# The out-projection of a hybrid encoder step: product halves in sequence, transpositions between them

## The chip, the cores and the metric

The kernel runs on one core of a Trainium2 chip. A core has five engines with one in-order queue each: TensorE (matmuls and transpositions, PE in the profile), VectorE (DVE), ScalarE (ACT), GpSimd (POOL) and SyncE (SP), which here issues all the DMAs. Matmul results land in PSUM, which has eight banks of 128 x 512 f32 values; ScalarE and VectorE carry them out of it. The metric is the device time of one execution in microseconds (us), as the median over runs.

## The reference, cut to what matters

One layer of a streaming encoder is applied to 1024 prompt frames and to 32 frames of a running stream, 1056 tokens of 1024 features. A mixer with three groups of heads (GLA, HGRN2, mLSTM) gives the concatenation `cat`; the out-projection, a norm, the residual, and a feed-forward block with a causal convolution follow:

```python
def run_trunk(x, states, params):                      # one layer, cut
    h, st_new = mixer(rms_norm(x, g_mix_pre[l]), ...)
    x = x + rms_norm(h, g_mix_post[l])
    h, ffn_buf = conv_ffn(rms_norm(x, g_ffn_pre[l]), ...)
    x = x + rms_norm(h, g_ffn_post[l])

def mixer(...):                                        # its end
    cat = jnp.concatenate([o_a, o_b, o_c], axis=-1)    # (B, T, 1024)
    return cat @ w_out, (...)                          # w_out (1024, 1024)

def conv_ffn(xn, buf, w_up, conv_w, conv_b, w_down):
    up = xn @ w_up
    up, buf = causal_dwconv(up, buf, conv_w, conv_b)
    gate, val = jnp.split(up, 2, axis=-1)
    return (jax.nn.gelu(gate, approximate=True) * val) @ w_down, buf
```

The recurrences of the three head groups run along the tokens, in chunks of 64; the new states are outputs too.

## The kernel before, in words

**Tiles of tokens.** The 1056 tokens form nine tiles: 0 to 7 with 128 tokens of the prompt each, and 8 with the 32 tokens of the running stream. The in-projection works in three groups, (0, 1, 2), (3, 4, 5) and (6, 7, 8). A matmul of two f32 operands is done as three matmuls of rounded high and low parts (`mm3`, lines 99 to 102), so one product of a token tile with a 1024 x 1024 matrix is 2 halves of 512 columns x 8 blocks of 128 rows x 3 = 48 matmuls.

**Mixers as side work.** `mixer` (line 704) is a generator: it traces the recurrences of one tile in some 15 steps, many small instructions on all engines, and yields between them. The mixers of a group run beside the stage that follows. `pump(k)` (line 1437) lets the side work advance by k steps; `merge(main, nmain, nside)` (line 1445) runs a main generator and, at each of its yields, pumps so many steps that nside steps are traced after nmain yields. The mixers of the last group, in the order 8, 6, 7, run beside the out-projection of the tiles 0, 1, 2, 3, 8, 4, 5 (`RING`, line 259). Each mixer needs the state of the one before it and shares its buffers, and writes its `cat` tile to DRAM; tile 7 keeps its own in SBUF.

**The out-projection of a tile.** `outproj` (line 1007) is a generator with four stages. The first loads the tile's cat (`load_cat`, line 261, tile ct) and residual (`load_res`, line 270, tile xr), and those of the next tile as well; it transposes cat into two PSUM banks, four blocks of 128 x 128 each (ctp, line 1031), and carries each out as a high part by ScalarE (ch, line 1035) and a low part by VectorE (cl, line 1036). These two have a raised priority. The second makes the product into two banks zp, block by block with the two halves alternating, and then ScalarE reads each bank twice, for the sum of squares (line 1066) and for a copy into the tile z (line 1067). The third is the norm, on GpSimd, VectorE and ScalarE (lines 1069 to 1086): scale by the norm and a gain (line 1076), add the residual (line 1077), store the sum (line 1078), square it (line 1081), scale again (line 1086). The fourth transposes the result into two banks (fxt, line 1100), which VectorE carries out with a gain (line 1105), and stores it for the up-projection (line 1108). Tile 0 also splits the out-projection's weights between its blocks (`out_weights`, line 994). The tiles 6 and 7 come after the others and have orders of their own.

**Buffers.** All of ctp, zp and fxt of the tiles 0 to 5 and 8 take their banks from one PSUM pool of three (`psb`, line 117). The tiles ct, xr and z of these tiles take theirs from a ring of seven slots in SBUF (`NRING`, line 256).

**The order.** `pipeline` (line 1113) takes the stages of successive tiles in turn: at place i the first stage of tile i, the fourth of the tile two places before, the third of the tile one place before, the second of tile i, with a yield behind each. A planner then sets the order of the instructions on each engine when the program is built: it follows the order of tracing as priority, its own estimates of durations, and the free buffers; a block under `tc.high_priority` counts as traced so much sooner. On the chip each engine then executes its list in that order.

**What follows.** Behind the out-projection come the up-projection (puy, pux, puw), whose operands VectorE and ScalarE prepare from the stored columns (T1l, B22l and others, line 1133), and the down-projection.

Of the kernel before, what the change touches and what calls it, by code (L numbers as in the profile page):

```python
# [8 lines left out]
F32 = mybir.dt.float32  # L9
# [3 lines left out]
AF = mybir.ActivationFunctionType  # L13
# [77 lines left out]
def body(ctx: ExitStack, tc: tile.TileContext, a: dict):  # L91
    nc = tc.nc
    act, dve, pool, pe, sp = nc.scalar, nc.vector, nc.gpsimd, nc.tensor, nc.sync
# [5 lines left out]
    def mm3(ps, lh, rh, first, last, **kw):  # L99
        pe.matmul(ps, lh[0], rh[0], start=first, stop=False, **kw)  # L100
        pe.matmul(ps, lh[0], rh[1], start=False, stop=False, **kw)  # L101
        return pe.matmul(ps, lh[1], rh[0], start=False, stop=last, **kw)  # L102
# [14 lines left out]
    psb = ctx.enter_context(tc.tile_pool(name="psb", bufs=3, space=PSUM))  # L117
# [25 lines left out]
    def xsrc(t0, n):  # L143
        return a["xp"][t0:t0 + n, :] if t0 < SEQ else a["xs"][t0 - SEQ:t0 - SEQ + n, :]
# [862 lines left out]
    def outproj(p2, W, u):  # L1007

        gm, woh, wol = W[:3]
        n = 128 if u < 8 else DEC  # L1010
        t0 = 128 * u
        load_cat(u)
        if u in RING:
            load_res(u)
            nxt = (RING + (6,))[RING.index(u) + 1]
            load_cat(nxt)
            if nxt in RING:
                load_res(nxt)
        ct = ct_of[u]
        chs = []  # L1020
        for hf in range(2):
            if u < 7 or u == 8:
                ps = psb.tile([128, 4, 128], F32, tag="big", name=f"ctp{u}{hf}")
            else:
# [3 lines left out]
                ps = both[:, hf]  # L1028
# [8 lines left out]
            if u == RING[0]:  # L1037
                halves[:] = ins
            chs += [(ch[:, k, :n], cl[:, k, :n]) for k in range(4)]
        yield  # L1040
        ss = p2.tile([128, 4], F32, tag="oss", name=f"oss{u}", bufs=2)
        pss = [psb.tile([128, 512], F32, tag="big", name=f"zp{u}{hf}") if u != 7 else
               upper[0].tile([128, 512], F32, tag="xw", name=f"zp{u}{hf}", bufs=4) for hf in range(2)]
        cs = [slice(512 * hf, 512 * hf + 512) for hf in range(2)]
        if u == 7:

            jk = jks[0]
            for hf in range(2):
                for k in range(8):
                    mm3(pss[hf], chs[k], (woh[:, k, cs[hf]], wol[:, k, cs[hf]]), k == 0, k == 7)  # L1050
                with tc.high_priority(offset=AHEAD):
                    kept["jk"] = act.activation(jk, pss[hf], AF.Square, accum_out=ss[:, hf:hf + 1])
        else:
            for k in range(8):
                if u == RING[0]:
                    next(W[3])
                for hf in range(2):
                    mm3(pss[hf][:n], chs[k], (woh[:, k, cs[hf]], wol[:, k, cs[hf]]), k == 0, k == 7)
                if k == 3 and u == 6:
                    yield  # L1060
        load_res(u)
        x = xr_of[u]
        if u != 7:
            z = (ring if u in RING else tail)[0](f"z{u}")
            for hf in range(2):
                act.activation(z[:n, cs[hf]], pss[hf][:n], AF.Square, accum_out=ss[:n, hf:hf + 1])
                act.copy(z[:n, cs[hf]], pss[hf][:n])
# [11 lines left out]
        if u == 7:  # L1079
            z = tail[0]("z7")  # L1080
# [356 lines left out]
    def pump(k):  # L1437
        while k > 0 and side:
            try:
                next(side[0])  # L1440
                k -= 1
            except StopIteration:
                side.pop(0)

    def merge(main, nmain, nside):

        done = 0
        for i, _ in enumerate(main):
            want = (i + 1) * nside // nmain
            pump(want - done)  # L1450
            done = want
# [6 lines left out]
    NMIX, NIN = 17, 12 + 2 + 24  # L1458
# [243 lines left out]
```

## Time and profile before

| | |
|---|---|
| time, median of 3 runs | 1419.99 us (1419.96 to 1420.18) |
| the profiled execution, its own time | 1421.18 us |
| its span | 1419.4 us |
| TensorE busy | 1368.0 us, 96% of the span |
| VectorE busy | 1009.2 us, 71% |
| ScalarE busy | 711.3 us, 50% |
| GpSimd busy | 281.9 us, 20% |

The profile is of one execution. Its page gives the busy time of each engine, groups of instructions by line, and the chain of waits. A row of a group reads: line, engine, operation, names of output and inputs, shapes, count, busy time, mean duration, idle time of the engine in front and what ended it. A row of the order in time reads: start, duration, engine, line, operation, names, and in brackets the idle time in front with its releaser. "x48" is a count. Line 1066 is the activation of line 1066; `mm3` gives the lines 100, 101 and 102, and `split` the lines 106 and 109, whoever calls them. The durations of matmuls overlap, so steps between starts tell the rate. The granted clock is that of TensorE as a share of full speed.

### The profile page before, as it was taken

To read this page: it belongs to the slowest core of one execution; us is meant where nothing else is said; L and a number is where in the kernel's file an instruction comes from. 1 tells how busy PE (TensorE), PEld (TensorE's weight loads), DVE (VectorE), ACT (ScalarE), POOL (GpSimd) and SP (SyncE) were. 2 spreads that over 40 slices of the span, in tenths; PEclk is the share of its full clock that TensorE was granted. 3 is DMA by queue.
4 is the path that set the end of the run, shared out by engine and by line. 5 is a ranking of instruction groups with operands and counts; after the bars stand their busy time and mean duration, and the time that the engine had idled before them with its cause. 6 is when DMAs were issued, how large, how long until landed. Compare 5 with 4: busy or idle time off the path is not lost.

```text
span 1419.4 us, 30029 instructions
## 1 busy us (share of the span) xinstructions
PE 1368.0 (96%) x11804; PEld 1253.1 (88%) x11804; DVE 1009.2 (71%) x1818; ACT 711.3 (50%) x1403; POOL 281.9 (20%) x461
## 2 busy tenths in 40 slices
PE   6989999999999998899899999999999999999998
PEld 5989889998888876767799999999999999988886
DVE  4795469758687667676798887788888875654644
ACT  4555447445474545333755545554455544533432
POOL 5531211224112223212131111111111110000100
PEclk9999999999999989999999999999999999999999
DMA  9599779776789753344412221221222156765652
GB/s 344 191 338 342 242 238 309 232 254 210 270 281 341 256 179 125 129 145 102 138 50 99 79 91 70 91 76 73 79 82 85 62 199 239 235 221 169 245 176 100
DMA packets 132581, 255.11 MB, mean 180 GB/s; under 512 B 27639, under 2 KB 78487, under 8 KB 132439
## 3 DMA queue, kind: packets, MB, share of 16 engines
q1 hardware_dynamic: 132439, 253.19, 52.3%
q8 instruction: 92, 1.51, 0.4%
q14 instruction: 50, 0.41, 0.1%
HBM read 192.26 MB, written 60.89 MB: 178 GB/s over the span
## 4 chain that ended last, share of the span: by engine, by line
PE 78%; DVE 8%; DMA 5%; ACT 4%; issue 2%; POOL 2%; SPq 1%; DVEq 0%; POOLq 0%; ACTq 0%
PE pd L102 6%; PE pd L101 6%; PE pd L100 6%; PE pux L100 4%; PE pux L102 4%; PE pux L101 4%; PE pv L100 3%; PE pv L102 3%; PE pv L101 3%; PE puw L101 3%; PE puw L100 3%; PE puw L102 3%; PE zp L100 2%; PE pf L100 2%; PE pf L101 2%; PE zp L101 2%
## 5 line engine op out<-in xcount | busy, mean ns | idle before, releaser
L1276 DVE SCALAR_TENSOR_TENSOR y<-uu,fconv_sb,y 128x1060 f32<-128x1060 f32 x88 | 116.2, 1321 | 28.5 <-ACT y L1274 27.8
L102 PE MATMUL pd<-wd,hl 128*128 128x512 f32 x264 | 105.0, 399 | 0.0
L101 PE MATMUL pd<-wd,hh 128*128 128x512 f32 x264 | 104.1, 394 | 0.0
L100 PE MATMUL pd<-wd,hh 128*128 128x512 f32 x264 | 103.5, 393 | 0.0
L1270 POOL COPY uu<-uu 128x2 f32<-128x2 f32 x44 | 36.6, 831 | 214.2 <-DVE uu L1218 214.0
L1213 ACT COPY c<-pux 128x274 f32<-128x274 f32 (+1 forms) x132 | 49.3, 376 | 40.8 <-PE pux L102 39.5
L1274 ACT ACTIVATE y<-uu,fconv_sb 128x1060 f32<-128x1060 f32 x44 | 56.1, 1275 | 16.9 <-POOL uu L1271 15.6
L100 PE MATMUL zp<-woh,ch 128*128 128x512 f32 (+1 forms) x144 | 59.1, 414 | 5.3 <-DVE z L1105 5.2
L100 PE MATMUL pv<-wt_0h,xh 128*128 128x256 f32 (+2 forms) x195 | 58.6, 301 | 5.6 <-ACT xh L318 5.4
L101 PEld LDWEIGHTS pd<-wd,hh 128*128 128x128 f32 x264 | 49.6, 188 | 12.6
L100 PEld LDWEIGHTS pd<-wd,hh 128*128 128x128 f32 x264 | 49.6, 188 | 11.7
L102 PEld LDWEIGHTS pd<-wd,hl 128*128 128x128 f32 x264 | 49.6, 188 | 11.5
L101 PE MATMUL zp<-wol,ch 128*128 128x512 f32 (+1 forms) x144 | 58.4, 405 | 0.0
L102 PE MATMUL pv<-wt_0h,xl 128*128 128x256 f32 (+2 forms) x195 | 57.6, 296 | 0.4 <-DVE xl L319 0.4
L102 PE MATMUL zp<-woh,cl 128*128 128x512 f32 (+1 forms) x144 | 57.6, 403 | 0.0
L101 PE MATMUL pv<-wt_0l,xh 128*128 128x256 f32 (+2 forms) x195 | 57.2, 293 | 0.1
L100 PE MATMUL pv<-wt_1h,xh 128*128 128x256 f32 (+2 forms) x195 | 56.8, 291 | 0.0
L102 PE MATMUL pv<-wt_1h,xl 128*128 128x256 f32 (+2 forms) x195 | 56.7, 291 | 0.0
L101 PE MATMUL pv<-wt_1l,xh 128*128 128x256 f32 (+2 forms) x195 | 56.5, 290 | 0.0
L100 PE MATMUL pd<-hh,wd 128*128 128x288 f32 x176 | 52.0, 296 | 0.0
L101 PE MATMUL pd<-hl,wd 128*128 128x288 f32 x176 | 52.0, 296 | 0.0
L102 PE MATMUL pd<-hh,wd 128*128 128x288 f32 x176 | 51.8, 296 | 0.0
(1678 smaller groups left out, 5138.6 us busy)
## 6 DMA issues: line engine op xcount, KB each, us to landing
h_d<-y SPq DMA_DIRECT2D x22, 530.0 KB, 2.7
wt_0r<-in_w_tok SPq DMA_DIRECT2D x21, 512.0 KB, 6.1
wt_1r<-in_w_tok SPq DMA_DIRECT2D x21, 512.0 KB, 6.5
wt_0l<-lt_d SPq DMA_DIRECT2D x14, 512.0 KB, 7.1
wt_1l<-lt_d SPq DMA_DIRECT2D x14, 512.0 KB, 7.6
hr<-h_d SPq DMA_DIRECT2D x44, 128.0 KB, 3.1
hr<-h_d SPq DMA_DIRECT2D x22, 192.0 KB, 3.2
x<-in_xp SPq DMA_DIRECT2D x8, 512.0 KB, 7.6
```

Of the source, the lines that this page charges most:

```text
L100: pe.matmul(ps, lh[0], rh[0], start=first, stop=False, **kw)
L101: pe.matmul(ps, lh[0], rh[1], start=False, stop=False, **kw)
L102: return pe.matmul(ps, lh[1], rh[0], start=False, stop=last, **kw)
L1213: kept[name] = act.copy(t, ps)
L1270: pool.tensor_copy(u[:, GAP_P:GAP_P + 2], u[:, GAP_S - 2:GAP_S])
L1274: act.activation(y, u, AF.Identity, scale=fconv[:, j, 2:3], bias=fconv[:, j, 3:4])
L1276: dve.scalar_tensor_tensor(y, uu[i][:, s:s + NCOL], fconv[:, j, s:s + 1], y, op0=ALU.mult, op1=ALU.add)
```

## The change

In `outproj`, for the tiles 0, 1, 2, 3, 8, 4, 5:

- a yield stands behind each of the two banks of transpositions (ctp) instead of behind both;
- the first stage loads the next tile's cat only; the tile's own residual is loaded ahead of its product, and no residual is loaded for the next tile;
- but for tile 0, the product is traced half by half: the eight blocks of columns 0 to 511 into a bank, ScalarE's two reads of it, a yield, then the same for columns 512 to 1023. Tile 0 keeps the alternating halves, since the weights are split between its blocks.

The tiles 6 and 7 keep their orders, but that the residual load of tile 6 is traced behind ScalarE's reads of its product. In `pipeline`, a place is now: half 0 of tile i, the first bank of transpositions of tile i + 1, half 1 of tile i, then the second bank of transpositions of tile i + 1, the fourth stage of tile i - 1 and the norm of tile i. In front of it all, tile 0 is transposed. The number of yields goes from 27 to 29, and the first number given to `merge` from 27 to 26, while the second stays at 3 x 17 + 2 = 53.

```diff
         load_cat(u)
         if u in RING:
-            load_res(u)
-            nxt = (RING + (6,))[RING.index(u) + 1]
-            load_cat(nxt)
-            if nxt in RING:
-                load_res(nxt)
+            load_cat((RING + (6,))[RING.index(u) + 1])
...
             chs += [(ch[:, k, :n], cl[:, k, :n]) for k in range(4)]
-        yield
+            if u in RING:
+                yield
+        if u not in RING:
+            yield
+        if u in RING:
+            load_res(u)
...
+        def bank(hf):
+            return psb.tile([128, 512], F32, tag="big", name=f"zp{u}{hf}") if u != 7 else \
+                upper[0].tile([128, 512], F32, tag="xw", name=f"zp{u}{hf}", bufs=4)
+
+        def product(ps, hf, k):
+            mm3(ps[:n], chs[k], (woh[:, k, cs[hf]], wol[:, k, cs[hf]]), k == 0, k == 7)
+
+        def leave(ps, hf):
+            act.activation(z[:n, cs[hf]], ps[:n], AF.Square, accum_out=ss[:n, hf:hf + 1])
+            act.copy(z[:n, cs[hf]], ps[:n])
+
+        if u == RING[0]:
+            pss = [bank(hf) for hf in range(2)]
+            for k in range(8):
+                next(W[3])
+                for hf in range(2):
+                    product(pss[hf], hf, k)
+            z = ring[0](f"z{u}")
+            for hf in range(2):
+                leave(pss[hf], hf)
+            yield
+        elif u in RING:
+            z = ring[0](f"z{u}")
+            for hf in range(2):
+                ps = bank(hf)
+                for k in range(8):
+                    product(ps, hf, k)
+                leave(ps, hf)
+                if not hf:
+                    yield
...
-            for k in range(8):
-                if u == RING[0]:
-                    next(W[3])
-                for hf in range(2):
-                    mm3(pss[hf][:n], chs[k], (woh[:, k, cs[hf]], wol[:, k, cs[hf]]), k == 0, k == 7)
-                if k == 3 and u == 6:
-                    yield
         load_res(u)
         x = xr_of[u]
-        if u != 7:
-            z = (ring if u in RING else tail)[0](f"z{u}")
-            for hf in range(2):
-                act.activation(z[:n, cs[hf]], pss[hf][:n], AF.Square, accum_out=ss[:n, hf:hf + 1])
-                act.copy(z[:n, cs[hf]], pss[hf][:n])
         yield
...
     def pipeline(gens):
-        for i in range(len(gens) + 2):
-            for j in (i, i - 2, i - 1, i):
-                if 0 <= j < len(gens) and i - 1 < len(gens):
-                    next(gens[j])
-                    yield
+        next(gens[0])
+        next(gens[0])
+        yield
+        for i, x in enumerate(gens):
+            after = gens[i + 1:i + 2]
+            next(x)
+            yield
+            for y in after:
+                next(y)
+            yield
+            next(x)
+            yield
+            for y in after + gens[i - 1:i] + [x]:
+                next(y)
+            yield
...
-    merge(pipeline(firsts), 27, 3 * NMIX + 2)
+    merge(pipeline(firsts), 26, 3 * NMIX + 2)
```

More of the change, by code (lines that the diff above doesn't have):

```diff
@@ L1039, in outproj @@
             chs += [(ch[:, k, :n], cl[:, k, :n]) for k in range(4)]
-        yield
+            if u in RING:
[4 more added lines that the diff above has]
+            load_res(u)
         ss = p2.tile([128, 4], F32, tag="oss", name=f"oss{u}", bufs=2)
-        pss = [psb.tile([128, 512], F32, tag="big", name=f"zp{u}{hf}") if u != 7 else
-               upper[0].tile([128, 512], F32, tag="xw", name=f"zp{u}{hf}", bufs=4) for hf in range(2)]
         cs = [slice(512 * hf, 512 * hf + 512) for hf in range(2)]
-        if u == 7:
+        def bank(hf):
[25 more added lines that the diff above has]
+                    yield
+        elif u == 6:
+            pss = [bank(hf) for hf in range(2)]
+            for k in range(8):
+                for hf in range(2):
+                    product(pss[hf], hf, k)
+                if k == 3:
+                    yield
+            z = tail[0](f"z{u}")
+            for hf in range(2):
+                leave(pss[hf], hf)
+        else:
+            pss = [bank(hf) for hf in range(2)]
             jk = jks[0]
@@ L1049, in outproj @@
                 for k in range(8):
-                    mm3(pss[hf], chs[k], (woh[:, k, cs[hf]], wol[:, k, cs[hf]]), k == 0, k == 7)
+                    product(pss[hf], hf, k)
                 with tc.high_priority(offset=AHEAD):
                     kept["jk"] = act.activation(jk, pss[hf], AF.Square, accum_out=ss[:, hf:hf + 1])
-        else:
-            for k in range(8):
-                if u == RING[0]:
-                    next(W[3])
-                for hf in range(2):
-                    mm3(pss[hf][:n], chs[k], (woh[:, k, cs[hf]], wol[:, k, cs[hf]]), k == 0, k == 7)
-                if k == 3 and u == 6:
-                    yield
         load_res(u)
         x = xr_of[u]
-        if u != 7:
-            z = (ring if u in RING else tail)[0](f"z{u}")
-            for hf in range(2):
-                act.activation(z[:n, cs[hf]], pss[hf][:n], AF.Square, accum_out=ss[:n, hf:hf + 1])
-                act.copy(z[:n, cs[hf]], pss[hf][:n])
         yield
@@ L1113, in pipeline @@
     def pipeline(gens):
-        for i in range(len(gens) + 2):
-            for j in (i, i - 2, i - 1, i):
-                if 0 <= j < len(gens) and i - 1 < len(gens):
-                    next(gens[j])
-                    yield
+        next(gens[0])
[12 more added lines that the diff above has]
+                next(y)
+            yield
     def col_operands(pool_, q, s, between=lambda: None):
```

## The prediction

> **What bounds the kernel now.** I read the page first, then the busy time by stretches, then the order on TensorE, ScalarE and VectorE around one tile boundary, and last the chain of waits there. The profiled execution spans 1419.4 us. The product that the change touches (zp) is the costliest TensorE group of its stage, and the page gives it an idle time in front that VectorE ends:
>
> ```profile
> span 1419.4 us, 30029 instructions
> L100 PE MATMUL zp<-woh,ch 128*128 128x512 f32 (+1 forms) x144 | 59.1, 414 | 5.3 <-DVE z L1105 5.2
> ```
>
> The out-projection runs from 521 us to about 690 us. By stretches (start:end, length, busy time of each engine, then the granted clock, DMA share, GB/s):
>
> ```profile
> 521.00:690.00 169.00, 157.59 (x1452) 121.46 (x1451) 124.46 (x245) 75.78 (x170) 43.49 (x67) 0.97 0.45 142
> 541.00:552.00 11.00, 11.00 (x51) 9.06 (x50) 10.88 (x22) 4.65 (x10) 7.46 (x7) 1.00 0.25 98
> 552.00:561.30 9.30, 6.36 (x111) 4.83 (x109) 9.30 (x22) 8.64 (x24) 3.83 (x4) 1.00 0.42 127
> 575.00:580.60 5.60, 4.07 (x83) 3.07 (x81) 3.20 (x5) 3.31 (x8) 0.93 (x3) 1.00 0.29 100
> 596.50:605.40 8.90, 6.55 (x98) 5.05 (x97) 8.72 (x22) 4.38 (x12) 3.97 (x6) 0.92 0.14 40
> 605.40:620.00 14.60, 14.60 (x142) 7.51 (x141) 12.95 (x37) 6.30 (x16) 1.25 (x3) 0.93 0.55 173
> 620.00:626.30 6.30, 4.88 (x93) 3.95 (x90) 5.44 (x13) 3.76 (x10) 3.24 (x6) 1.00 0.68 248
> 638.50:647.00 8.50, 7.43 (x143) 6.11 (x142) 5.64 (x11) 5.38 (x12) 2.25 (x7) 1.00 0.21 79
> ```
>
> TensorE idles 169.00 - 157.59 = 11.4 us. The stretch 541 to 552 is the product of the second tile, without a gap. The five short stretches (552, 575, 596.5, 620, 638.5) lie between the product of one tile and that of the next. Their idle time is 2.94 + 1.53 + 2.35 + 1.42 + 1.07 = 9.31 us: nearly all of it. What happens there, on TensorE, then ScalarE:
>
> ```profile
> 551.80 0.39 PE L102 MATMUL zp<-woh,cl 128*128 128x512 f32 x1
> 552.03 0.49 PE L1031 MATMUL ctp<-ident,ct 128*128 128x128 f32 x3
> 554.60 0.66 PE L1031 MATMUL ctp<-ident,ct 128*128 128x128 f32 x4
> 556.63 1.04 PE L1100 MATMUL fxt<-ident,z 128*128 128x128 f32 x8
> 561.35 0.50 PE L100 MATMUL zp<-woh,ch 128*128 128x512 f32 x1 [2.92 <-DVE z L1105]
> 551.54 0.60 ACT L1066 ACTIVATE z<-zp 128x512 f32<-128x512 f32 x1 [4.14 <-PE zp L102]
> 552.04 0.19 ACT L1066 ACTIVATION_READ_ACCUMULATOR z<-zp 128x1 f32 x1
> 552.26 0.58 ACT L1067 COPY z<-zp 128x512 f32<-128x512 f32 x1
> 552.75 0.60 ACT L1066 ACTIVATE z<-zp 128x512 f32<-128x512 f32 x1
> 554.00 0.56 ACT L1035 CAST ch<-ctp 128x512 fp32r<-128x512 f32 x1
> 555.23 0.58 ACT L1067 COPY z<-zp 128x512 f32<-128x512 f32 x1
> 556.34 0.57 ACT L1035 CAST ch<-ctp 128x512 fp32r<-128x512 f32 x1
> ```
>
> Both halves of a product end together, so ScalarE drains two banks in a row while the transpositions of the next tile (ctp) have only begun. The second ctp waits until 554.60 for a bank, its cast starts at 556.34, and the next product starts at 561.35, 9.3 us behind the last matmul. The chain of waits through that boundary runs over ScalarE and VectorE, not TensorE:
>
> ```profile
> 551.54 0.70 ACT z L1066 x2
> 560.69 0.60 DVE z L1105
> 561.29 0.60 DVE cl L1036
> ```
>
> **The change part by part.** Nothing is added or removed: the same 48 matmuls, 16 transpositions, four drains and the same DMAs per tile. What moves:
>
> (1) Halves one behind the other (tiles 1, 2, 3, 8, 4, 5; the first tile keeps its interleaved product, and the tiles 6 and 7 keep theirs). Half 0 ends about 5.5 us before half 1 (half of the 11.0 us stretch), and its drain, 0.60 + 0.19 + 0.58 = 1.4 us, lies under half 1. Behind the tile only half 1's 1.4 us is left, where two drains stand now.
>
> (2) The first ctp of the next tile goes between the halves, the second behind half 1 with the fxt of the tile before. Transposing between products is in the trace already, in tile 6:
>
> ```profile
> 671.64 0.39 PE L102 MATMUL zp<-woh,cl 128*128 128x512 f32 x1
> 671.87 0.60 PE L1031 MATMUL ctp<-ident,cat 128*128 128x128 f32 x4
> 672.23 0.48 PE L100 MATMUL zp<-woh,ch 128*128 128x512 f32 x1
> 672.54 0.40 PE L101 MATMUL zp<-wol,ch 128*128 128x512 f32 x1
> 678.28 0.48 PE L100 MATMUL zp<-woh,ch 128*128 128x512 f32 x1
> 561.22 0.67 DVE L1036 TENSOR_TENSOR cl<-ctp,ch 128x512 fp32r<-128x512 f32 x1
> ```
>
> From 671.64 to 672.54 are 0.90 us for what is two steps of about 0.23 us without it (551.80 to 552.03 is one): 0.44 us for four transpositions, no more than they take in the gap. TensorE's sum stays.
>
> What is left at a boundary: behind half 1, TensorE has one ctp (0.60) and eight fxt (1.04), 1.6 us of work. The next half 0 needs a bank: the one of that ctp is free after cast 0.57 and subtraction 0.67 (the last row), some 1.9 us behind half 1, or 2.4 us if ScalarE's Square stands in front. So 0.3 to 0.8 us idle, and up to one long VectorE instruction more (1.2 us, L1077 below). The lower end is 0, where mixer matmuls fill it; the upper end is today's mean, 9.31 / 5 = 1.86 us. I take 0.6, which lies nearest to the rows of the drains. Saved: 9.31 - 5 x 0.6 = 6.3 us.
>
> (3) Loads. The cat load of the next tile is issued about half a tile earlier than now, the residual a whole tile later, at the start of its own product. On SP's queue it moves behind a tile's mixer loads and behind the x2 store, which can hold the queue:
>
> ```profile
> DMA to landing us min/median/max: 2.6/4.7/7.5
> SPq L1078 <- DVE xr L1077: 25.3, 6, 13.7
> 562.89 1.21 DVE L1077 TENSOR_TENSOR xr<-z,xr 128x1024 f32<-128x1024 f32 x1
> ```
>
> The first user of the residual (L1077) ran 11.35 us behind the product's end (562.89 against 551.54). With 11 us of product in front, a load of at most 7.5 us is hidden even behind the longest hold of 13.7 us (21.2 against 22 us). Cost 0; without that cover the norm would be late, and its fxt with it, and then the in-order TensorE. One ring slot less is held per tile, which can only free loads. Tile 6's residual load goes behind its drain in the order of tracing, with nothing else of SP's in between: 0.
>
> (4) Mixers. Three mixers, 14 + 15 + 15 = 44 steps, are traced beside the seven tiles, 53/27 = 1.96 per yield now and 53/26 = 2.04 after. Ahead of the product of the tiles in places 3, 4, 5 (from 0) stand 4i yields now, so 23, 31, 39 steps; after, 1 + 4i ahead of half 0, so 26, 34, 42, and two yields, four steps, more ahead of half 1. The mixers gain three to seven steps of 44 in priority. No instruction more; on TensorE their work is 35.4 us of the stage (first row: the sum over its stretches of the mixers' line 702 alone):
>
> ```profile
> sum 169.00, PE 35.42 PEld 28.66; mean PE 4.43 PEld 3.58
> 659.06 0.49 DVE L965 TENSOR_TENSOR hn<-hn,om 128x325 f32<-128x325 f32 x1 [3.41 <-PE om L702]
> 603.45 0.90 PE L702 MATMUL om<-vm,w 64*64 64x65 f32 x20 [2.35 <-DVE w L927]
> 664.85 0.49 DVE L904 TENSOR_TENSOR cat<-hn,hrs 128x320 f32<-128x320 f32 x1 [0.20 <-POOL hrs L219]
> ```
>
> The last mixer waits 3.41 us on TensorE near its end, where it stands behind a product. Sooner tracing helps there. I count it at 0, because even if it stays put the end is safe: its cat is complete at about 666.4 (664.85 + 0.49 and one product on POOL, about 1 us), and transposing, cast and subtraction (0.60 + 0.57 + 0.67) would let the last tile's product start at 668.3; it starts at 678.3 now (row above). That leaves 10 us of room for a gain of 6.3.
>
> (5) The end. The up-projection follows; its operands come from VectorE:
>
> ```profile
> 685.90 1.30 DVE L1133 TENSOR_TENSOR T1l<-xg,T1h 128x1096 fp32r<-128x1096 f32 x1 [0.51 <-ACT T1h L1132]
> 690.80 0.29 PE L100 MATMUL puw<-T1h,S_0h 128*128 128x274 f32 x1
> ```
>
> T1l is ready at 687.2 for a use at 690.8: 3.6 us of margin. It starts from the columns of tile 4, whose fxt stands behind tile 5's product and moves with it. So I count no loss; if it did not move, the gain would be capped at 3.6.
>
> **The sum.** 1421.18 us of the profiled execution less 6.3 gives 1414.9; that execution is 1.2 us above the median of the runs, 1419.99, so against the median 1413.7 us.
>
> **A rule weighed.** Clock: after 605.4 the stretch shows 0.93, behind one of 0.92 with 2.35 us idle, but the stretch with most idle time (2.94) and the product behind it show 1.00. The Trainium skill, "TensorE: Matmul & The Clock Gate", in its table on why this matters, wants no idle gaps beyond about 3 us lest the clock halve; here the dip came with less. The same page, "A second HAM failure mode", speaks against this change: cycling through PSUM banks at 512 columns can make the clock swing. The rows of 671.64 to 672.54 change bank twice at full step, which does not bear it out; its price is a rival below.
>
> **The rivals.**
> - Gap closed wholly: mixer matmuls fill the boundaries, and the dip goes too. 9.31 us plus 8.9 x 0.08 + 14.6 x 0.07 = 1.7 us gives 11.0, so 1409 us. For it: 35 us of mixer work to fill with. Against: VectorE is full (9.30 of 9.30) in the worst boundary.
> - Given back at the start of the up-projection: 3.6 us at most, 1416.4 us. For it: T1l's margin. Against: its source moves too.
> - The change does not do what it says: three banks and a full VectorE hold the next product as now, idle time only changes place. About 1420 us. For it: the subtraction at 561.29 stood in a VectorE queue, not on ScalarE.
> - Slower, by the order on TensorE: the planner sets mixer matmuls by its own estimates ahead of products, and where VectorE is late the products behind them wait, as at 603.45 (2.35 us, the one large case now). It decides from four such stalls on: 4 x 2.35 = 9.4 against 6.3, so 1423 us; six give 1428. For it: mixers gain priority, VectorE is busy 124 of 169 us. Against: of some dozens of such meetings one is large today.
> - Slower, by the clock: a dip as that of 596.5 to 620 costs 1.7 us. One more behind each of the five boundaries takes 8.7, more than the 6.3 saved: 1422.4 us. Against: the product of 541 to 552 changes banks all the time at 1.00. By the page's rule on bank cycling this would come.
>
> **How the numbers follow.** Forecast 0.50 (1410.7 to 1417.2), wholly closed 0.13, given back 0.07, no effect 0.11, stalls 0.15, clock 0.04. The predicted time is the forecast's, 1413.7. A measurement tells about 0.2%, 2.8 us, from no change. Faster by more: 0.50 + 0.13 + 0.07 = 0.70; within: 0.11; slower: 0.19. The range reaches from 1407.5 (most of the wholly closed case) to 1424 (no effect and four stalls); 0.05 below and 0.11 above are left out. The forecast's own range is 1410.7 (residual 0) to 1417.2 (residual 1.3 us, a long VectorE instruction in each boundary).
>
> **What would show it.** ScalarE should drain half 0 (Square and copy) in the middle of a tile's product; the idle time of zp behind L1105 (5.2 us) should fall under 2 us; TensorE idle in the stage should be 4 to 6 us instead of 11.4, and the stage 6 us shorter; the last mixer's cat should not land later. Wrong if new waits of zp or of mixer matmuls on VectorE appear, if the clock falls under 0.95, or if the last product starts as early as forecast and puw waits for T1l.

## The result, and the profile after

The changed kernel takes 1415.82 us (median of 21 runs, 1410.89 to 1421.92); beside it, in the same set, the kernel before took 1421.87 (1417.51 to 1426.69). The ratio is 0.996, with a 95% interval of 0.9951 to 0.9969: 6 us faster. The forecast was 6.3 us off the time before, so the size came out. The reason given for it did not, as the experiments show; that the size agrees is luck.

The profiled execution after took 1410.89 us, 10.3 us less than the one before. Single executions of either kernel lie up to 5 or 6 us to either side of their median, and part of these 10.3 us stands ahead of the change: the last matmul of the input projection (pv) starts at 510.76 us before and at 506.24 after. The traces are therefore compared from the first matmul of the first out-projection product on, which starts at 521.04 before and 516.52 after, in both 10.28 us behind that pv.

The page of the kernel after, the span and the zp group that carried the idle time:

```profile
span 1409.1 us, 30033 instructions
L100 PE MATMUL zp<-woh,ch 128*128 128x512 f32 (+1 forms) x144 | 59.0, 412 | 1.4 <-DVE z L1136 1.2
```

The idle time that VectorE ended in front of zp fell from 5.2 to 1.2 us (L1136 is what was L1105). By stretches, after: the stage as a whole, then the five boundaries between tile products that answer to the prediction's five (columns as there):

```profile
516.50:677.50 161.00, 156.53 (x1450) 121.16 (x1449) 124.10 (x245) 75.24 (x170) 44.47 (x67) 0.98 0.48 149
549.80:552.60 2.80, 2.80 (x53) 2.69 (x52) 1.70 (x6) 2.18 (x6) 1.24 (x4) 1.00 0.07 25
565.80:568.60 2.80, 2.80 (x66) 2.41 (x65) 1.73 (x3) 1.65 (x4) 0.93 (x3) 1.00 0.02 4
585.00:590.30 5.30, 4.10 (x70) 2.96 (x69) 5.12 (x13) 2.94 (x8) 2.11 (x4) 1.00 0.21 62
607.80:610.70 2.90, 2.90 (x54) 2.75 (x52) 2.90 (x8) 2.23 (x6) 2.24 (x5) 1.00 0.02 6
624.60:632.30 7.70, 6.67 (x137) 5.54 (x135) 3.58 (x10) 1.96 (x5) 0.75 (x2) 1.00 0.06 19
```

The stage holds the same work (1450 matmuls against 1452). It is 161.0 us long instead of 169.0, and TensorE idles 4.5 us in it instead of 11.4. Three of the boundaries have no idle time at all, the other two 1.2 and 1.0 us: 2.2 us in all, where there were 9.31. The boundary behind the second tile, on TensorE and then on ScalarE:

```profile
549.59 0.39 PE L102 MATMUL zp<-woh,cl 128*128 128x512 f32 x1
549.82 0.60 PE L1027 MATMUL ctp<-ident,ct 128*128 128x128 f32 x4
550.26 0.96 PE L702 MATMUL mi<-cf_sb,x 128*128 128x11 f32 x8
551.14 0.69 PE L702 MATMUL sc<-Qz,Ld 64*64 64x64 f32 x32
551.76 1.09 PE L1131 MATMUL fxt<-ident,z 128*128 128x128 f32 x8
552.61 0.48 PE L100 MATMUL zp<-woh,ch 128*128 128x512 f32 x1
...
544.08 0.58 ACT L1054 ACTIVATE z<-zp 128x512 f32<-128x512 f32 x1
544.78 0.59 ACT L1055 COPY z<-zp 128x512 f32<-128x512 f32 x1
550.37 0.57 ACT L1054 ACTIVATE z<-zp 128x512 f32<-128x512 f32 x1
551.41 0.57 ACT L1055 COPY z<-zp 128x512 f32<-128x512 f32 x1
```

Half 0 is drained at 544.08, in the middle of the product, as forecast. The reader is also to see the two rows of line 702 between the ctp and the fxt: 40 matmuls of a mixer, ready to run just when the product has nothing. They turn out to matter more than the drain.

Behind the stage a little is given back. The 30 us from the end of the last out-projection product on, first before, then after:

```profile
690.00:720.00 30.00, 23.62 (x146) 21.08 (x145) 23.70 (x28) 21.44 (x42) 8.29 (x11) 0.89 0.27 75
```

```profile
678.00:708.00 30.00, 22.59 (x138) 21.04 (x137) 23.73 (x28) 20.92 (x40) 7.87 (x13) 0.83 0.24 75
```

TensorE does about 8 fewer matmuls in the same 30 us: 1.0 us more idle, and a granted clock of 0.83 instead of 0.89. So about 8 us are gained in the stage, and 1 to 2 go again at the start of the up-projection.

### The profile page after: what moved, and what is told of

The parts are those of the page before. It is cut to its first block, busy times and chain, and to the rows that moved or that the text cites. A ratio compares the mean times of both kernels' runs of the same rounds, so it can differ in the third digit from the quotient of the medians.

```text
span 1409.1 us, 30033 instructions
## 1 busy us (share of the span) xinstructions
PE 1362.5 (97%) x11804; PEld 1248.9 (89%) x11804; DVE 1008.6 (72%) x1818; ACT 711.5 (50%) x1403; POOL 278.9 (20%) x461
## 4 chain that ended last, share of the span: by engine, by line
PE 74%; DVE 9%; DMA 7%; ACT 5%; issue 3%; POOL 2%; SPq 1%; DVEq 0%; POOLq 0%; ACTq 0%
PE pd L102 6%; PE pd L101 6%; PE pd L100 6%; PE pux L100 4%; PE pux L102 4%; PE pux L101 4%; PE puw L100 3%; PE puw L101 3%; PE puw L102 3%; PE pf L100 3%; PE pf L101 2%; PE pf L102 2%; PE zp L102 2%; PE zp L100 2%; PE zp L101 2%
## 5 line engine op out<-in xcount | busy, mean ns | idle before, releaser
L1312 POOL COPY uu<-uu 128x2 f32<-128x2 f32 x44 | 29.7, 674 | 212.3 <-DVE uu L1260 212.2
L1316 ACT ACTIVATE y<-uu,fconv_sb 128x1060 f32<-128x1060 f32 x44 | 56.1, 1275 | 17.3 <-POOL uu L1313 15.9
L102 PEld LDWEIGHTS pd<-wd,hl 128*128 128x128 f32 x264 | 49.6, 188 | 11.4
```

The source lines that it names most:

```text
L1312: pool.tensor_copy(u[:, GAP_P:GAP_P + 2], u[:, GAP_S - 2:GAP_S])
L1316: act.activation(y, u, AF.Identity, scale=fconv[:, j, 2:3], bias=fconv[:, j, 3:4])
```

## The experiments

Each kernel ran beside the kernel before on the same chip. The median of the latter was 1422.07 us beside the kernels with 29, with 25, with ctp behind both halves and with alternating halves, 1421.86 beside those with alternating halves and ctp behind, with the late mixers that catch up, with 24 in the kernel before and with the early residual, and 1422.40 beside the other four; the first row of the change in the table is from its own set above.

A measure that stood up better than any single wait is how many matmuls TensorE has behind it a fixed time after the first zp. The work of each kernel is the same, so a count ahead is time ahead. The mark of 132 us is near the end of the last product of the ring (the tiles of `RING`) in the change, 131.7 us. At 200 us all are in the up-projection, which runs about 8.5 matmuls a microsecond where nothing holds it (67 or 68 in 8 us from 721 us on, before). All runs:

```
kernel                       ratio to before    matmuls by  matmuls by  TensorE idle
                             (95% interval)     132 us      200 us      by 132 us
before                       1                  1222        1604        11.2
the change                   0.996  .9951-.9969 1311        1660         3.2
the change again             0.9943 .9923-.9963 1302        1647         2.8
mixers back (29)             1.0013 .9997-1.0028 1240       1605         4.5
before, mixers sooner (25)   1.0114 1.0094-1.0134 1196      1536        13.5
before, mixers sooner (24)   1.0044 1.0026-1.0062 1182      1562        10.9
ctp behind both halves       0.9958 .9944-.9972 1303        1658         5.5
halves alternating           0.992  .9902-.9938 1318        1665         3.7
halves alternating, again    0.9902 .9881-.9922 1318        1691         4.0
alternating, ctp behind      0.997  .9952-.9988 1292        1640         6.9
mixers in their old places   1.0002 .9986-1.0017 1239       1577         5.7
mixers late, then catching up 0.998 .9961-.9999 1247        1629         5.1
alternating, mixers 24       0.996  .9942-.9977 1314        1624         4.3
residual loaded early        0.9951 .993-.9973  1275        1621         3.1
```

The count of the change at 200 us is 56 ahead, 56 / 8.5 = 6.6 us, and the runs gave 6.05. In "before, mixers sooner (24)" it is 42 behind, 4.9 us, and the runs gave 7.2. It is not exact for a single trace (the start of the stage scatters by some 3 us, see the last section), but the order of the kernels is nearly that of the runs (the one with the residual loaded early is the main exception). The column by 132 us parts them into two groups, from 1182 to 1247 and from 1275 to 1318: every kernel of the second group is faster than before, and of the first only the one that catches up late is, by 0.2%. What parts them are the mixers. By the profile's groups of lines they have 880 matmuls in the stage (line 702), and by 132 us all 880 are done in seven of the eight traces of the second group, 860 in that with the residual loaded early, and 808 to 832 in the six of the first. Of the 89 matmuls by which the change leads the kernel before there, 62 are the mixers' and 22 the products'.

**The mixers put back.** The prediction counted them at nothing. The change with its mixers traced about as late as before (the counts are in the text below; the change has 26, 34 and 42 there). The mixers have 44 steps, so the 53 of `merge` are never reached, and in every kernel here the last step is traced ahead of the last of the ring's products: with 26 behind half 0 of the sixth tile of the ring, with 29 ahead of half 0 of the seventh. Where texts below speak of 45, 48, 50 or all 53 steps by the end of the ring, they count against that 53 and name steps that don't exist; what the number sets is how soon each step is traced.

```diff
-    merge(pipeline(firsts), 26, 3 * NMIX + 2)
+    merge(pipeline(firsts), 29, 3 * NMIX + 2)
```

> The changed kernel with merge's first number 29 in place of 26: ahead of half 0 of the tiles in places 3, 4 and 5 stand 23, 31 and 38 mixer steps, as before the change (23, 31, 39). Only the sooner tracing of the mixers is undone. Halves in sequence make the gain: ratio to the kernel before 0.995 to 0.997, TensorE idle in the stage 4 to 6 us. Mixers traced sooner make it: ratio 0.999 to 1.001, idle 9 us or more.

1423.57 us, ratio 1.0013 (0.9997 to 1.0028). The whole gain is gone, although the halves, the early transposition and the loads are as in the change. TensorE idles 6.6 us from the first zp to the last, not the 9 or more that the text had for this case: idle time fell without a gain in time. Two rows of this kernel, the first 132 us, and the stretch between the ring's last product and that of tile 6:

```profile
521.90:653.90 132.00, 127.50 (x1240) 95.94 (x1239) 95.61 (x201) 55.82 (x131) 35.38 (x52) 0.97 0.48 145
652.40:661.72 9.32, 7.60 (x93) 5.95 (x92) 7.72 (x18) 3.19 (x9) 5.74 (x9) 0.82 0.40 121
```

and the same two of the change:

```profile
516.50:648.30 131.80, 128.63 (x1309) 98.06 (x1308) 99.73 (x215) 56.29 (x132) 39.03 (x56) 0.98 0.47 146
648.20:651.10 2.90, 2.38 (x20) 1.91 (x18) 2.01 (x4) 2.14 (x6) 1.69 (x5) 1.00 0.00 0
```

The ring's products end 130.5 us behind the first zp here, 131.7 in the change and 140.3 in the kernel before: the halves do their work. But 73 matmuls of the mixers are not done by then. They stand on TensorE ahead of tile 6's product, which starts 9.3 us behind the ring's last product instead of 2.9. VectorE's last write of the last mixer's cat (L904) starts at 146.7 us instead of 136.6, and the last matmul of tile 7's product at 166.2 instead of 160.2.

**The mixers alone.** The kernel before, with nothing but the number changed:

```diff
-    merge(pipeline(firsts), 27, 3 * NMIX + 2)
+    merge(pipeline(firsts), 25, 3 * NMIX + 2)
```

> The kernel before with merge's first number 25 in place of 27: 25, 33 and 42 mixer steps ahead of the products in places 3, 4 and 5, as the change has ahead of half 0 (26, 34, 42). Only the mixers are moved. Halves in sequence make the gain: ratio 0.999 to 1.001, idle 10 to 12 us. Mixers traced sooner make it: ratio 0.995 to 0.997.

1436.37 us, ratio 1.0114 (1.0094 to 1.0134): much slower, which neither theory had. To see whether that was an accident of one order, the same with 24, by which 26, 35 and 44 steps stand ahead of the products in places 3, 4 and 5:

```diff
-    merge(pipeline(firsts), 27, 3 * NMIX + 2)
+    merge(pipeline(firsts), 24, 3 * NMIX + 2)
```

> The kernel before with merge number 24 in place of 27, and nothing else: 50 of the 53 mixer steps are traced by the end of its 23 pipeline steps, as many as in the change (45 with 27; 48 with 25, which took 1.0114). Theory A (in the old order of the pipeline sooner mixers stand in front of the products' own work: each long wait of TensorE is followed by some microseconds at a lower clock, so the loss is systematic): ratio 1.006 to 1.020, with at least four slices of 8 us at a granted clock of 0.75 to 0.85 in the stage. Theory B (the 1.0114 of 25 is an accident of one order that the planner found, and sooner mixers are worth about 7 us by themselves): ratio 0.994 to 1.000.

1429.06 us, ratio 1.0044 (1.0026 to 1.0062). The size depends on the order that the planner finds, the sign does not: theory A, a little below its range (five slices of 8 us lie at a clock of 0.57 to 0.83). The first 132 us of the stage, with 25:

```profile
521.50:653.50 132.00, 118.44 (x1196) 87.72 (x1194) 92.37 (x200) 53.86 (x126) 31.35 (x49) 0.94 0.42 138
```

and with 24:

```profile
520.20:652.20 132.00, 121.09 (x1182) 89.92 (x1180) 90.04 (x193) 51.52 (x119) 30.87 (x45) 0.93 0.41 135
```

Sooner mixers make the old order slower in two ways. Idle time stays (13.6 and 10.9 us, against 11.2 in the kernel before), now spread over many waits. And the clock falls to 0.94 and 0.93, against 0.96. The waits of TensorE in the stage with 25 name products, transpositions and mixers alike:

```profile
PE zp L102 <- DVE cl L1036: 3.6, 2, 1.9
PE mi L702 <- DVE kw L937: 3.0, 3, 1.9
PE ctp L1031 <- ACT z L1067: 1.9, 3, 0.9
PE fxt L1100 <- DVE cl L1036: 1.7, 2, 1.0
PE mi L702 <- ACT kt L781: 1.6, 2, 1.1
```

**The halves and the transposition undone, one by one and together.** First both sets of transpositions of the next tile behind half 1:

```diff
-            for y in after:
-                next(y)
             yield
             next(x)
             yield
-            for y in after + gens[i - 1:i] + [x]:
+            for y in after + after + gens[i - 1:i] + [x]:
```

> The changed kernel with both transpositions of the next tile behind half 1; halves in sequence stay. The drain and the early transposition each carry part: ratio 0.997 to 0.9985, with zp or ctp waits of 3 to 5 us back in the boundaries. The early drain of half 0 alone carries the gain: 0.996. The transposition between the halves alone carries it: 0.9995 to 1.001.

1415.36 us, ratio 0.9958 (0.9944 to 0.9972): the same as the change. By the text above this leaves the early drain of half 0 as the carrier; the next run takes that away too. Then the halves alternating, with the first set in the middle of the product:

```diff
-            for hf in range(2):
-                ps = bank(hf)
-                for k in range(8):
-                    product(ps, hf, k)
-                leave(ps, hf)
-                if not hf:
+            pss = [bank(hf) for hf in range(2)]
+            for k in range(8):
+                for hf in range(2):
+                    product(pss[hf], hf, k)
+                if k == 3:
                     yield
+            for hf in range(2):
+                leave(pss[hf], hf)
```

> The changed kernel with the two halves alternating as before, and the first transposition of the next tile behind block 3 of 8; both drains are behind the product again. The drain carries a large part, since the next product needs two free banks at once and ScalarE empties two (2.6 us): ratio 0.998 to 1.000. The transposition in the middle alone carries the gain: 0.996.

1408.91 us, ratio 0.992 (0.9902 to 0.9938): better than the change, which none of the cases had. The two edits together, so that neither named idea is left:

> The change without both of its named ideas: the halves of a product alternate block by block as before, and both sets of transpositions of the next tile are issued behind the product. What is left is the new order of the rest of the pipeline (the drain and the norm of the previous tile), the earlier own-input loads and the mixers at merge number 26. Theory A (neither the sequence of the halves nor the place of the transpositions carries the gain, since each was undone alone without loss: 0.992 and 0.9958 of the kernel before): both undone together still gain, ratio 0.990 to 0.997. Theory B (each of the two covers for the other: with the halves alternating both drains stand behind the product, and only transpositions issued early hide them, so that with both undone the five gaps of 9.3 us between the tile products return): ratio 0.998 to 1.003 and about 9 us of TensorE idle ahead of the tile products.

1417.10 us, ratio 0.997 (0.9952 to 0.9988): 4.8 us faster than before, theory A, at the upper end of its range. Side by side, the four kernels are at 0.996 (early) and 0.9958 (behind) with halves in sequence, and at 0.992 and 0.997 with alternating ones. So the early transposition is worth nothing beside halves in sequence, but some 8 us beside alternating halves, and beside the early transposition the sequence of the halves costs some 7 us. What the four share gives 5 of the 6 us of the change.

In the kernel without both, both drains stand behind the product once more, one after the other, and the transpositions wait for them as in the kernel before. Its boundary behind the third tile, and the busy time of the eight microseconds from there:

```profile
571.98 0.60 ACT L1054 ACTIVATE z<-zp 128x512 f32<-128x512 f32 x1 [5.70 <-PE zp L102]
572.47 0.60 PE L1027 MATMUL ctp<-ident,ct 128*128 128x128 f32 x4
573.00 0.69 PE L702 MATMUL sc<-Qz,qkb 64*64 64x64 f32 x32
573.19 0.60 ACT L1054 ACTIVATE z<-zp 128x512 f32<-128x512 f32 x1
573.62 0.92 PE L702 MATMUL mi<-v,kt 128*32 128x64 f32 x22
574.47 0.66 PE L1027 MATMUL ctp<-ident,ct 128*128 128x128 f32 x4
574.96 1.04 PE L1132 MATMUL fxt<-ident,z 128*128 128x128 f32 x8
576.00 0.33 PE L702 MATMUL og<-v,P 64*64 64x64 f32 x4
...
579.87 0.50 PE L100 MATMUL zp<-woh,ch 128*128 128x512 f32 x1
```

```profile
572.00:580.00 8.00, 8.00 (x184) 6.92 (x183) 5.61 (x8) 4.68 (x12) 0.93 (x3) 1.00 0.30 101
```

The same eight microseconds behind that product in the kernel before:

```profile
575.20:583.20 8.00, 6.41 (x93) 5.03 (x93) 5.80 (x8) 3.11 (x8) 0.93 (x3) 1.00 0.45 158
```

This pair shows the mechanism at this boundary. The next zp does not come sooner: it starts 7.4 us behind the first ctp (579.87 - 572.47), against 5.2 before (580.65 - 575.48). But TensorE is busy 8.00 of 8.00 us with 184 matmuls, against 6.41 us with 93, because the scores, states and outputs of a mixer are ready to be run there. The gap was not shortened. It was filled.

**The places of the mixers' steps.** What the kernel with neither idea still shares with the change is where the pipeline hands over to the mixers. Before, one yield stands behind each of the transpositions, the fxt, the norm and the product, so mixer steps are traced between them. In the change they are traced twice in the middle of a product (behind half 0 and behind the first bank of transpositions), once behind it and once behind the norm; the second bank, the fxt and the norm follow one another. The kernel below takes the two hand-overs out of the product and puts one behind the second bank and one behind the fxt; in both kernels one stands between the product and the second bank. The change, with its halves, its early transposition and its 26, and only these places put back:

```diff
-            next(x)
-            yield
-            for y in after:
-                next(y)
-            yield
-            next(x)
+            for y in [x] + after + [x]:
+                next(y)
             yield
-            for y in after + gens[i - 1:i] + [x]:
+            for y in after:
                 next(y)
             yield
+            for y in gens[i - 1:i]:
+                next(y)
+            yield
+            next(x)
+            yield
```

> The change with its halves in sequence, its transposition between the halves, its loads and its merge number 26, but with the mixer's steps traced where the kernel before has them: none within a tile's product, and one each behind the product, behind the next tile's transpositions, behind the previous tile's transposition of x and behind the norm. Theory A (what the change brings is that no mixer step is traced between a product's drain and the next tile's transpositions, norm and transposition of x, so that these come ahead of it in every queue; in the old places 48 and 50 steps took 1.0114 and 1.0044): ratio 1.002 to 1.012, and fewer than 1250 matmuls by 132 us behind the first product, against 1311 in the change. Theory B (the sequence of the halves and the early transposition shelter the products, wherever the mixers are traced): ratio 0.994 to 0.998 and about 1300 matmuls.

1423.65 us, ratio 1.0002 (0.9986 to 1.0017). The gain is gone again. The 1239 matmuls by 132 us are as theory A had them; the time is just under its range, as there is no loss beyond the gain:

```profile
521.30:653.30 132.00, 126.35 (x1239) 95.39 (x1238) 96.62 (x206) 54.66 (x127) 39.54 (x54) 0.95 0.46 141
```

The last write of the last mixer's cat starts at 150.1 us, 13.5 later than in the change, though as many steps are traced at each yield. So two things are needed together, and each undone alone takes the gain: the new places, and mixers traced sooner. In the kernel before, sooner mixers cost 7 and 14 us. In the new places they bring about 7 (0.996 against 1.0013). The new order of the fxt and the norm is in this kernel too, so it isn't enough by itself; whether the places and the rate would do without it, no run shows.

**Must they be sooner all along, or only done by the end?** The slow rate for the first 20 yields, then the rate of the change, so that from yield 21 on as many steps are traced as there:

```diff
             want = (i + 1) * nside // nmain
+            if late is not None and i >= late:
+                want = (i + 1) * nside // 26
...
-    merge(pipeline(firsts), 26, 3 * NMIX + 2)
+    merge(pipeline(firsts), 29, 3 * NMIX + 2, 20)
```

> The change with the mixers traced at the slow rate of merge number 29 for the first 20 of the 25 steps of the pipeline, and at the rate of 26 for the last five, so that they are as far as in the change when the ring products end (50 of 53 steps, against 45 with 29 throughout). With 29 throughout the gain was gone (1.0013): 132 us behind the first product TensorE had done 1240 matmuls, against 1309 in the change, and the 69 were done behind the ring's products. Theory A (what counts is how much of the mixers is left behind the ring's last product): ratio 0.994 to 0.998, and about 1300 matmuls by 132 us. Theory B (the rate throughout counts, for filling the early gaps): ratio 0.999 to 1.003.

1418.56 us, ratio 0.998 (0.9961 to 0.9999): at the edge of theory A's range, and the count that A named is missed (1247, not 1300). Somewhat over half of what the slow rate loses comes back (0.998, between 1.0013 and 0.996). So the early part of the rate and the late one seem both to count; how much each, this run doesn't settle.

**More still.** The alternating version with the mixers sooner yet (26 becomes 24, by which the last step is traced two yields sooner):

> The version with alternating halves and one set of transpositions in the middle of the product (0.992) with merge number 24, so that all 53 mixer steps are traced by the end of the ring's products. If a mixer left behind the products still costs there (its last matmuls, 92 between the ring's and the next tile's products), ratio 0.987 to 0.991; if the sooner steps now delay the products instead, 0.993 to 1.000.

1417.76 us, ratio 0.996 (0.9942 to 0.9977). Too soon: at 132 us the count is as good as with 26 (1314), but behind that TensorE waits for the copy out of a product's bank:

```profile
PE fxt L1132 <- ACT z L1055: 4.7, 2, 4.4
```

**The loads.** The residual of a tile loaded at its first stage again, as before:

```diff
         load_cat(u)
         if u in RING:
+            load_res(u)
             load_cat((RING + (6,))[RING.index(u) + 1])
```

> The change with the loads part undone: a tile's own residual input is loaded at its first stage again. Theory of the prediction (the loads cost and bring nothing): within 0.2 per cent of the change, ratio to before 0.994 to 0.998. Rival (the later load frees the queue for the mixer results and carries part of the gain): ratio 0.998 to 1.002.

1415.62 us, ratio 0.9951 (0.993 to 0.9973): no part of the gain.

**The better version and the change, once more side by side.** Both unaltered:

> The alternating version once more, beside the change itself on one chip, since its 0.992 came from six executions. If it is better than the change by itself, ratio to before 0.990 to 0.994; if that was scatter, 0.994 to 0.998 like the change.

> The change itself once more, unaltered, on the chip of the runs beside it: ratio 0.994 to 0.998 as before. Two profiled executions of one kernel also show how much of a difference between single traces is scatter of the granted clock: a span 3 to 5 us apart by the low clock around the first product alone (6.8 us at 0.50 in the change's trace, 13.6 in that of the kernel before).

1409.90 us (0.9902, 0.9881 to 0.9922) and 1416.67 us (0.9943, 0.9923 to 0.9963). The alternating version is the best kernel here, some 6.8 us below the change and 12.5 below the kernel before. In its two traces the last write of the last mixer's cat starts at 127.0 and 125.9 us, against 136.6 and 138.1 in those of the change, and between 132 and 200 us TensorE idles 7.4 and 6.8 us against 8.7 and 10.8. That the earlier cat is the cause was not tried by itself; with 24 it is earlier still (120.8), and that kernel is slower.

## Why the prediction was right, and where it was not

- **What bounds.** Right in part: the idle time between tile products was the thing to gain, 9.31 us of 11.4, and 6.9 of the 11.4 went. What ended the waits in the trace (the drains, then VectorE's subtraction) was read as what had to be shortened. The other side of it was passed over: a boundary costs nothing if TensorE has other work ready, and idle time taken out of a boundary is no gain if other work is still to be done behind it (with 29, 4.5 us by 132 us against 11.2 in the kernel before, and no gain).
- **Step (1), the halves.** The drain moved under half 1 as worked out, in most tiles; in the sixth place both Squares still came together (631.75 and 632.32). It isn't what made the time: with alternating halves and the early transposition the kernel is faster yet.
- **Step (2), the early transposition and 0.6 us left per boundary.** Measured 0, 0, 1.2, 0 and 1.0, a mean of 0.44, and 6.9 us saved in the stage against 6.3. The size is close, the attribution is wrong: with both transpositions behind the product the time is the same (0.9958), and with both steps in place but the mixers late there is no gain. So the agreement of 6.3 with 6.05 us is luck.
- **Step (3), the loads at 0.** Right: 0.9951 with that part undone.
- **Step (4), the mixers at 0.** This step failed. The argument was that the end is safe even if the last mixer stays put, as tile 7's product had 10 us of room behind its cat. The run with 29 is that case, and it isn't safe: the room was counted for the cat of tile 7, while the mixers' own matmuls stand on TensorE ahead of tile 6's product (73 of them, in a stretch of 9.3 us), and the ring's products, which end 9.8 us sooner than before, gain nothing. Nor are mixers only something that must be done in time: they are what fills the boundaries. Their rate alone undone takes the gain (1.0013), their places alone undone take it too (1.0002). The prediction counted steps gained in priority (three to seven of 44) and didn't ask between which of the pipeline's instructions they are traced.
- **Step (5), the end.** T1l starts at 674.41 and takes 1.29, so it is ready at 675.7 for a first use at 678.57: 2.9 us of margin, against 3.6. No loss there, as counted; but 1 to 2 us were given back behind it by other waits and the clock, a small case of the rival that capped the gain.
- **The rivals.** Gaps closed wholly: nearly so in the boundaries, for the reason that the rival gave, mixer matmuls filling them, though its time, 1409 us, didn't come. What weighed against it, a full VectorE, didn't hold the fill. Slower by mixer stalls: it didn't come in the change, but it is real, as the kernel before with sooner mixers shows (1.0044 and 1.0114). What parts the two is the place of the steps, which the prediction had no price for. Slower by the clock: no.
- **The rule weighed.** The prediction took the rule, which the page has from a bf16 kernel, to speak against the change; but halves in sequence stay in one bank for 24 matmuls, where alternating ones change bank after every three, so it would speak for it. Cycling through banks at 512 columns did not make the clock swing in either. The changed stage has 0.98, against 0.97 with the old order, and the alternating kernels aren't apart from it (0.97 in the first 132 us of both traces). No run here bears out the rule of the Trainium skill, "TensorE: Matmul & The Clock Gate", section "A second HAM failure mode", for such products.

What stays open is by which queue the old places hurt. That the steps traced between the transpositions, the fxt and the norm come ahead of what follows them fits the waits shown with 25, where ctp, fxt and zp all wait for ScalarE and VectorE. It was shown as an effect of the place, not at a single instruction. Nor is it idle time alone: by 200 us the change with the old places idles 14.2 us (11.9 in the change, 17.8 before), but by the profile's groups of lines the same 880 mixer matmuls keep TensorE busy for 52.0 us instead of 45.2, and the 432 of the products for 180.1 instead of 175.2.

## What to carry to other kernels

Where an in-order TensorE has a gap that a chain of other engines sets, first ask what independent work could stand there, and where in the order it is traced; filling the gap was worth more here than shortening the chain (4.8 us with neither named idea, nothing with both and late mixers). When a change brings several edits, price the smallest number in it too, and undo each alone and in pairs: here 29 for 26 undid everything, the early transposition was worth nothing beside one form of the product and 8 us beside the other. Count the matmuls done a fixed time behind a common mark; that told apart kernels whose idle times looked alike (1240 with 4.5 us idle and no gain, 1303 with 5.5 and a ratio of 0.9958).

## What the runs showed of the hardware

A low granted clock came in lengths of one quantum. Summed over windows of 1 us from 7 us ahead of the first zp to 200 us behind it, the fourteen traces have 59 stretches below full clock, and all last 3.4, 6.8, 10.2 or 13.6 us (to 0.1) at 0.50. A step of the product takes 0.43 us there (522.04 to 522.47 in the kernel before) against 0.23 at full clock, so each quantum costs, by an estimate, half of its 3.4 us, 1.7 us, if TensorE is busy through it. The Trainium skill, "TensorE: Matmul & The Clock Gate", section "What's actually happening", has a free-running window of about 3.4 us, and the lengths agree. The same section has everything behind the first 3.4 us or so of work run at full clock; the first trace below agrees, with the clock back after 3.1 us of unbroken work, and the second does not, with 7.5 us of it at 0.50.

The same wait ahead of the stage is followed by two quanta in some executions and by four in others, with one kernel, too. In the trace of the change the clock is back 3.1 us behind the first zp, after 6.8 us (two stretches and the rise, columns as above):

```profile
512.80:516.50 3.70, 2.15 (x9) 1.57 (x10) 3.09 (x7) 1.28 (x4) 1.12 (x2) 0.50 0.99 275
516.50:519.60 3.10, 3.10 (x12) 2.07 (x12) 1.92 (x8) 2.69 (x5) 0.33 (x1) 0.50 1.00 381
519.50:520.50 1.00, 1.00 (x12) 0.88 (x13) 0.97 (x2) 1.00 (x3) 0.00 (x0) 0.93 0.92 343
```

In its second trace it falls in the microsecond from 515 us and is back at 529, after 13.6 us, though TensorE is busy without a gap for the last 7.5 of them:

```profile
515.00:516.00 1.00, 1.00 (x10) 0.81 (x9) 0.39 (x1) 0.70 (x1) 0.28 (x2) 0.57 0.00 0
521.00:528.50 7.50, 7.50 (x28) 5.01 (x26) 6.36 (x14) 6.52 (x8) 2.25 (x2) 0.50 0.96 321
529.00:530.00 1.00, 1.00 (x11) 0.86 (x11) 1.00 (x2) 0.00 (x0) 0.00 (x0) 1.00 0.84 326
```

That is, by the estimate above, up to 3.4 us of time between two runs of the same instructions, a part of the scatter of single executions, and a reason not to read a gain of 3 us from two traces.
